# Setting up triangles in small parts between the state's steps, and two attention heads side by side on the array's columns

## The chip, the cores and the metric

The kernel runs on one core of one Trainium2 chip. The metric is the device time of one execution in microseconds (us); lower is better. A core has TensorE (PE; its weight loads are shown apart as PEld), VectorE (DVE), ScalarE (ACT), GpSimd (POOL) and SyncE (SP), which issues nearly all DMA transfers here. Each engine works through its own list of instructions in order.

## What is computed

Two layers over 2304 tokens (256 of context, 2048 latents on a grid 64 wide) of width 1024. In each layer a conditioning vector gives shift, scale and gate (`ada_modulation`); the normalised, modulated stream goes through one input projection into three groups of heads (A: gated delta rule, B: attention on a neighbourhood, C: gated linear attention), and their outputs, each gated, through one output projection.

```python
for i in range(DEPTH):
    sh, sc, gt = split(silu(c) @ w_mod[i] + b_mod[i])          # for c and for c_ctx
    m = layer_norm(x) * (1 + sc) + sh
    parts = split(m @ w_in[i])
    # group A, in chunks (of 64 tokens here, of 128 in the kernel), both directions, 4 heads of 128
    lmat = strict(k_beta @ k.T * decay);  u, w = solve(I + lmat, [v*beta, k_beta*exp(g)])
    for chunk: v_new = u - w @ S;  o = q_dec @ S + (q @ k.T * decay) @ v_new;  S = S * g_last + k_dec.T @ v_new
    # group B, 4 heads of 64: 8 x 16 window and 256 context keys
    p = softmax(concat(q @ k_window + bias, q @ k_ctx));  o = p @ concat(v_window, v_ctx)
    ...
    x = LN(alpha * x + gt * (concat(gated outputs) @ w_out[i]))
```

## The kernel before, in words

The tokens are 18 chunks of 128 (NT). Within a layer the stages stand in the program in this order: modulation (`stage_mod`, first layer only, with the first normalisation), a dense pass with group C, a dense pass for group B, a stage that makes tables and gates and the rest of the modulation vectors (`stage_mod` again: the gate row of this layer and, in layer 0, shift and scale of layer 1) together with two dense passes with a short convolution for group A, a dense pass for the gate of group A (here the *z pass*, lines 1260 and 1261), the delta rule with the attention, and the output projection.

`stage_mod` multiplies the two conditioning vectors (2 columns of weights, `e.cc`) with 512 columns of `w_mod` at a time: 8 matmuls per group of 512, four groups for shift and scale, two for the gate (line 104).

The delta rule (class `Gdn`) goes over the 4 heads in two pairs (`hp`) and over the chunks in both directions. Before a chunk can be used, its triangle has to be set up and inverted. This goes in batches of two groups of three chunks (`BATCHES`, three for each pair of heads, numbered 0 to 5): `prep` loads keys and decays, multiplies keys with keys and queries (line 849), and writes the triangle X and the matrix A (lines 853 to 860); `diagonal` takes the 32 x 32 blocks on the diagonals through DRAM, and inverts them by 30 eliminations, two VectorE instructions each (lines 913 and 914, a serial chain); `solve` loads the inverses back through DRAM, turns them (line 892) and puts the 128 x 128 inverse together on TensorE (`assemble`). Then `scan` runs steps: one *step* is one chunk in each direction for one pair of heads: state times keys (line 999), R (1003), X times R (1010), scale (1013), new part of the state (1017), state update (1022, or 1024 in the first step), output (1030, 1032). A step needs the state of the step before, so the 18 steps of a pair are a chain, and there are 36 steps in a layer.

`run` is a generator, advanced between the z pass and the two halves of the attention. Before the change it issues: prep 1, prep 2, solve 0 (then the z pass), then for k = 1 to 5 diagonal k and solve k as one piece, six steps, prep k+2; each piece in front of the steps that follow it.

The attention (class `Natten`) calls `attend` once for each 128 queries and pair of heads: 16 times in a pair for the latents, and, in layer 0, twice for the context: 68 times in all. The scores are evicted and made exponentials, transposed (lines 1229 and 1236), and multiplied with the values (line 1245): the transposed weights are the stationary operand (128 columns), 64 columns of v move, one head after the other, 2 + 4 products (2 + 3 at the upper and lower edge, 2 for the context) for each head. An fp32 matmul stands as two rows in the trace.

The order of instructions on each engine is made when the program is built: a list scheduler takes ready instructions, those that come earlier in the program first. So what is written earlier has the first claim on an engine, and later work (z pass, attention) fills what is left; on the chip each engine's order is then fixed.

Of the kernel before, what the change touches and what calls it, by code (L numbers as in the profile page):

```python
# [89 lines left out]
def stage_mod(e, pool, ps, tag, tt, bufs, w_mod, b_mod, modT, GT, parts, step):  # L90


    nc = e.nc
    w4 = w_mod.rearrange("(k p) n -> p k n", p=128)
    for n in parts:
        s = slice(512 * n, 512 * n + 512)
        b = pool.tile([2, 512], F32, tag="bm", name="b", bufs=2)
        nc.sync.dma_start(b, b_mod[s].partition_broadcast(2))
        p = ps.tile([2, 512], F32, tag=tag, name="p")
        for k in range(0, KD, step):  # L100
            w = pool.tile([128, step, 512], F32, tag="wm", name="w", bufs=bufs)
            nc.sync.dma_start(w, w4[:, k:k + step, s])
            for j in range(step):
                nc.tensor.matmul(p, e.cc[:, k + j], w[:, j], start=k + j == 0, stop=k + j == KD - 1)  # L104
        nc.vector.tensor_tensor(b, b, p, op=ALU.add)
        if n >= 4:
            nc.sync.dma_start(GT[:, 512 * (n - 4):512 * (n - 3)], b)
            continue
        pt = ps.tile([128, 4, 2], F32, tag=tt, name="pt")
        for j in range(4):  # L110
            nc.tensor.transpose(pt[:, j], b[:, j * 128:(j + 1) * 128], e.ident[0:2, 0:2])
        nc.vector.tensor_scalar(modT[:, 4 * n:4 * n + 4], pt, float(n >= 2), None, op0=ALU.add)
# [463 lines left out]
class Gdn:  # L576
# [179 lines left out]
    def start(self, ctx, dr, ps):  # L756
# [10 lines left out]
        self.XD[0] = self.prep(s, b, P, ps, "dn", ax)  # L767
        self.diagonal(P, *self.XD[0])
# [9 lines left out]
    def run(self):  # L778
# [5 lines left out]
        def prep(k):  # L784
            if k < len(self.BATCHES):
                hp, b = self.BATCHES[k]
                self.XD[k] = self.prep(self.st[hp], b, self.P1, self.ps, "pp", self.ax)

        def solve(k):
            hp, b = self.BATCHES[k]  # L790
            if k:
                self.diagonal(self.PM, *self.XD[k])
            self.solve(self.st[hp], b, *self.XD.pop(k))
# [7 lines left out]
        prep(1)  # L801
        prep(2)
        solve(0)
        yield
        for k in range(1, 6):
            solve(k)
            if k % 3:
                self.scan(self.st[k // 3], range(6 * (k % 3) - 6, 6 * (k % 3)))
            else:
                self.scan(self.st[k // 3 - 1], range(12, 18))  # L810
            prep(k + 2)
            if k == 3:
                yield
        self.scan(self.st[1], range(12, 18))
# [16 lines left out]
    def prep(self, s, batch, P, ps, tag, ax):  # L831
# [7 lines left out]
        for gi, g in enumerate(batch):  # L839
            A, X = zip(ax(), ax())  # L840
            for ci in range(3):
# [14 lines left out]
                for d in range(2):  # L856
# [3 lines left out]
                    nc.vector.tensor_tensor(A[d][:, ci], pk[:, :, 1], E[:, d], op=ALU.mult)  # L860
            for d in range(2):
# [15 lines left out]
        return n, LD, XD  # L877

    def diagonal(self, P, n, LD, XD):
# [4 lines left out]
        self.invert(P, M, n)  # L884
# [16 lines left out]
    def invert(self, P, M, n):  # L901
# [5 lines left out]
        for k in range(1, 31):  # L907
# [6 lines left out]
            nc.vector.tensor_tensor(o, o, tv, op=ALU.add)  # L914

# [50 lines left out]
    def scan(self, s, steps):  # L966
        nc = self.e.nc
        order = (list(range(NT)), [1, 0] + list(range(NT - 1, 1, -1)))
        for n in steps:
# [5 lines left out]
            for _ in zip(*both):  # L975
                pass
# [67 lines left out]
class Natten:  # L1044
# [162 lines left out]
    def attend(self, qs, keys, bias, nk, chunks, v, dst):  # L1207
# [25 lines left out]
        for a in range(2 if nk else 0):  # L1233
# [303 lines left out]
```

## Time and profile before

| | |
|---|---|
| time, median of 3 (lowest, highest) | 3989.75 us (3979.24, 4000.7) |
| profiled execution | 3995.01 us, its span 3992.9 us |
| busy PE, PEld, DVE, ACT, POOL | 91%, 78%, 63%, 42%, 20% |
| mean granted TensorE clock | 0.913 |
| DMA | 787.57 MB, mean 197 GB/s |

A busy PE means that a matmul is under way somewhere in the array's pipeline; a matmul's row is longer than the time until the next may start, so starts are compared, not durations. The granted clock is given as a share of full speed (1.0 is 2.4 GHz, 0.5 is 1.2 GHz). The layers are alike: layer 0 ends its delta rule and attention at 1794 us, layer 1 at 3745 us.

### The profile page before, as it was taken

What the parts mean: (1) busy time and instruction counts of PE and PEld (TensorE: products, weight loads), DVE (VectorE), ACT (ScalarE), POOL (GpSimd) and SP (SyncE); (2) the same over time, 40 slices, a digit from 0 to 9 for tenths busy, and PEclk for the clock granted to TensorE, in tenths of its full rate; (3) what the DMA queues carried; (4) which work ended last, traced back from release to release, by engine and by line L of the source; (5) the groups of instructions that cost most, each with busy time, mean ns of one, the idle gap of its engine ahead of it and who ended that gap; (6) DMA issues with size and microseconds to landing.
All of it is one profiled execution on the core that took longest, in us unless ns stands there. A gap on an engine that the chain in (4) does not pass through costs nothing.

```text
span 3992.9 us, 77074 instructions
## 1 busy us (share of the span) xinstructions
PE 3626.0 (91%) x27262; PEld 3113.1 (78%) x27262; DVE 2521.8 (63%) x7471; ACT 1660.0 (42%) x4387; POOL 810.2 (20%) x1182
## 2 busy tenths in 40 slices
PE   7999998899989999897898999999999898989788
PEld 3777787579977888896676778887998788879676
DVE  5465462668975676356875556527798766753587
ACT  4533231335433454446545333213454244545342
POOL 0121111210101332221232211112111132331133
PEclk8988988899999998898898888899999998988899
DMA  9843435876687876666647443268776887775753
GB/s 312 280 147 105 133 112 169 245 232 201 205 276 219 246 229 189 187 196 214 203 132 232 152 147 115 100 210 251 215 232 201 285 228 205 228 217 150 219 160 111
DMA packets 756088, 787.57 MB, mean 197 GB/s; under 512 B 190207, under 2 KB 665207, under 8 KB 755703
## 3 DMA queue, kind: packets, MB, share of 16 engines
q1 hardware_dynamic: 755702, 782.64, 63.6%
q8 instruction: 216, 3.54, 0.4%
q14 instruction: 170, 1.38, 0.1%
HBM read 548.41 MB, written 234.03 MB: 196 GB/s over the span
## 4 chain that ended last, share of the span: by engine, by line
PE 55%; DMA 19%; DVE 16%; ACT 4%; issue 3%; SPq 2%; POOL 0%; DVEq 0%; ACTq 0%; POOLq 0%
PE p L190 29%; DMA mm<-MS 3%; PE p L1245 3%; DMA gb<-GR 2%; PE p L104 2%; DMA kk<-KK 2%; DMA raw<-in_w_in 1%; PE py L190 1%; PE po L1030 1%; PE pk L999 1%; PE pv L1010 1%; DMA oa<-OA 1%; PE pd L1017 1%; PE pt L1236 1%; DVE y L1374 1%
## 5 line engine op out<-in xcount | busy, mean ns | idle before, releaser
L190 PE MATMUL p<-mm,wh 128*128 128x384 f32 (+1 forms) x3648 | 1004.0, 354 | 67.2 <-DMA mm<-MS 21.4
L190 PEld LDWEIGHTS p<-mm,wh 128*128 128x128 f32 (+1 forms) x3648 | 667.8, 192 | 133.7 <-DMA mm<-MS 36.9
L190 PE MATMUL p<-mm,wl 128*128 128x384 f32 (+1 forms) x1824 | 635.1, 350 | 1.8 <-DVE wl L182 1.8
L190 PE MATMUL p<-wh,mm 128*128 128x512 f32 (+1 forms) x1696 | 570.5, 409 | 14.5 <-DMA mm<-MS 4.9
L190 PEld LDWEIGHTS p<-wh,mm 128*128 128x128 f32 x1696 | 329.1, 197 | 92.0 <-DMA mm<-MS 8.4
L649 DVE SCALAR_TENSOR_TENSOR acc<-pre,cw,acc 128x384 f32<-128x384 f32 (+1 forms) x576 | 351.8, 629 | 39.2 <-ACT acc L647 35.8
L190 PEld LDWEIGHTS p<-mm,wl 128*128 128x128 f32 (+1 forms) x1824 | 348.9, 191 | 22.8 <-issue 14.6
L190 PE MATMUL p<-wl,mm 128*128 128x512 f32 (+1 forms) x848 | 341.5, 403 | 4.3 <-DVE wl L182 4.3
L190 PE MATMUL py<-wh,mh 128*128 128x512 f32 x544 | 221.7, 410 | 17.1 <-ACT mh L1360 13.2
L190 PE MATMUL py<-wh,ml 128*128 128x512 f32 x544 | 213.9, 405 | 8.7 <-DVE ml L1361 8.7
L190 PE MATMUL py<-wl,mh 128*128 128x512 f32 x544 | 217.8, 402 | 0.0
L190 PEld LDWEIGHTS p<-wl,mm 128*128 128x128 f32 x848 | 166.5, 196 | 38.5 <-DVE wl L182 4.8
L992 POOL TENSOR_TENSOR kd<-kk,eD 128x256 f32<-128x256 f32 x144 | 90.4, 628 | 476.4 <-DMA kk<-KK 225.6
L1224 ACT ACTIVATE w<-w,mn 128x696 f32<-128x696 f32 (+2 forms) x136 | 112.9, 830 | 143.9 <-DVE mn L1221 142.6
L1383 POOL TENSOR_TENSOR y<-y,g 128x1024 f32<-128x1024 f32 x32 | 77.5, 2423 | 416.0 <-ACT y L1382 416.0
L639 POOL COPY pre<-pre 128x4 f32<-128x4 f32 x120 | 75.0, 627 | 416.4 <-DVE acc L649 244.1
L913 DVE TENSOR_TENSOR tmp<-M 96x30 f32<-96x30 f32 (+4 forms) x360 | 127.1, 353 | 27.7 <-issue 11.3
L1245 PE MATMUL p<-v,wl 120*128 120x64 f32 (+1 forms) x960 | 141.1, 286 | 0.0
L853 DVE SCALAR_TENSOR_TENSOR gb<-gb,Gt,mats 128x128 f32<-128x128 f32 x288 | 86.7, 358 | 83.0 <-DMA gb<-GR 82.8
L1261 DVE SCALAR_TENSOR_TENSOR zt<-zt,p 128x256 f32<-128x256 f32 (+1 forms) x102 | 51.4, 506 | 138.8 <-ACT zt L1260 131.9
L190 PEld LDWEIGHTS py<-wh,mh 128*128 128x128 f32 x544 | 106.4, 196 | 41.4 <-ACT mh L1360 16.1
L914 DVE TENSOR_TENSOR M<-M,tmp 96x30 f32<-96x30 f32 (+4 forms) x360 | 130.4, 362 | 6.1
(307 smaller groups left out, 8021.8 us busy)
## 6 DMA issues: line engine op xcount, KB each, us to landing
mm<-MS SPq DMA_DIRECT2D x384, 384.0 KB
kk<-KK SPq DMA_DIRECT2D x144, 512.0 KB
MS<-mm SPq DMA_DIRECT2D x96, 384.0 KB
raw<-in_w_in SPq DMA_DIRECT2D x104, 256.0 KB
w<-in_w_mod SPq DMA_DIRECT2D x96, 256.0 KB
M<-m SPq DMA_DIRECT2D x36, 512.0 KB
mm<-M SPq DMA_DIRECT2D x96, 192.0 KB
KK<-kq SPq DMA_DIRECT2D x96, 192.0 KB
```

The lines of the kernel that those rows point to most:

```text
L104: nc.tensor.matmul(p, e.cc[:, k + j], w[:, j], start=k + j == 0, stop=k + j == KD - 1)
L190: e.nc.tensor.matmul(p, x(k), y(k), start=n == 0, stop=n == 3 * KD - 1)
L639: nc.gpsimd.tensor_copy(pre[:, 0:4], pre[:, m:m + 4])
L649: nc.vector.scalar_tensor_tensor(acc[:, :n], pre[:, k:k + n], w(kind, k), acc[:, :n], op0=ALU.mult, op1=ALU.add)
L853: nc.vector.scalar_tensor_tensor(E[:, d, h], gb[:, d, h], self.G[:, d, c, h0 + h:h0 + h + 1], e.mats[:, 1 + d], op0=ALU.subtract, op1=ALU.min)
L913: nc.vector.tensor_tensor(tv, col, row, op=ALU.mult)
L914: nc.vector.tensor_tensor(o, o, tv, op=ALU.add)
L992: nc.gpsimd.tensor_tensor(kd, kv[:, :, 0], self.eD[:, d, c, h0:h0 + 2].unsqueeze(2).to_broadcast([128, 2, 128]), op=ALU.mult)
L1224: nc.scalar.activation(w[:, a, 0:256 + nk], w[:, a, 0:256 + nk], AF.Exp, bias=m[:, a:a + 1], scale=-1.0, accum_out=sm[:, a:a + 1])
L1245: nc.tensor.matmul(p[:, a], l, r, start=j == 0, stop=j == len(parts) - 1)
L1261: nc.vector.scalar_tensor_tensor(th[:, :n], th[:, :n], 1.0, z, op0=ALU.add, op1=ALU.mult)
L1383: eng.tensor_tensor(y[:, s], y[:, s], self.g[:, 0, s], op=ALU.mult)
```

## The change

Three things change. (1) `scan` takes generators of other work and advances them between the sub-steps of its steps; `prep` yields after each chunk, and `invert` after each elimination, so that both are spread over the steps. The batches stand earlier in the program: the first three steps, with diagonal 1 between them, are issued before the z pass. (2) In `attend` the values are the stationary operand, 64 columns for each head, and the two heads' products stand side by side on the array's columns (tile positions 0 and 64), with 128 moving columns; the result comes out transposed, is copied by ScalarE and transposed back by one more matmul. (3) `stage_mod`, not named in the title, puts up to four groups of 512 on column positions 0, 32, 64 and 96, loads two groups by one transfer of 512 KB with half as many buffers, and finishes with one set of full transposes.

```diff
-    for n in parts:
-        s = slice(512 * n, 512 * n + 512)
...
-                nc.tensor.matmul(p, e.cc[:, k + j], w[:, j], start=k + j == 0, stop=k + j == KD - 1)
...
+    for k in range(KD):
+        for i0 in range(0, n, 2):
+            w = pool.tile([128, 2, 512], F32, tag="wm", name="w", bufs=bufs)
+            nc.sync.dma_start(w, w4[:, k, 512 * (n0 + i0):512 * (n0 + i0) + 1024].rearrange("p (i c) -> p i c", i=2))
+            for i in range(i0, i0 + 2):
+                nc.tensor.matmul(p[32 * i:32 * i + 2], e.cc[:, k], w[:, i - i0], start=k == 0, stop=k == KD - 1, tile_position=(0, 32 * i))
+    for i in range(n):
+        r = slice(32 * i, 32 * i + 2)
+        nc.vector.tensor_tensor(b[r], b[r], p[r], op=ALU.add)
...
@@ class Gdn, run
-        prep(1)
-        prep(2)
+        run = lambda *g: [None for x in g for _ in x]
+        run(prep(1))
         solve(0)
+        self.scan(self.st[0], range(3), diag(1))
+        run(prep(2))
         yield
-        for k in range(1, 6):
-            solve(k)
-            if k % 3:
-                self.scan(self.st[k // 3], range(6 * (k % 3) - 6, 6 * (k % 3)))
-            else:
-                self.scan(self.st[k // 3 - 1], range(12, 18))
-            prep(k + 2)
-            if k == 3:
-                yield
-        self.scan(self.st[1], range(12, 18))
+        solve(1)
+        self.scan(self.st[0], range(3, 6), diag(2))
+        solve(2)
+        self.scan(self.st[0], range(6, 12), prep(3), diag(3))
+        self.scan(self.st[0], range(12, 18), prep(4), diag(4))
+        yield
+        solve(3)
+        self.scan(self.st[1], range(3), prep(5))
+        solve(4)
+        self.scan(self.st[1], range(3, 6), diag(5))
+        solve(5)
+        self.scan(self.st[1], range(6, 18))
         yield
...
@@ invert, after each elimination; prep, after each chunk
+            yield
...
-    def scan(self, s, steps):
+    def scan(self, s, steps, *work):
+        parts = (x for w in work for x in w)
+        share = -(-48 // len(steps))
...
-            for _ in zip(*both):
-                pass
+            for i, _ in enumerate(zip(*both)):
+                if i:
+                    for _ in range(share // 6):
+                        next(parts, None)
+        for _ in parts:
+            pass
...
@@ attend
+        p = ps.tile([128, 128], F32, tag="t", name="p", bufs=2)
+        parts = [(128, lambda a, j=j: (self.vc[:, j], wc[:, a, j])) for j in range(2)] + [(k, lambda a, j=j, k=k: (v[:k, j], wl[a][:k, j])) for j, (_, k) in enumerate(chunks)]
+        for j, (k, f) in enumerate(parts):
+            for a in range(2):
+                c = slice(64 * a, 64 * a + 64)
+                l, x = f(a)
+                nc.tensor.matmul(p[c], l[:, c], x, start=j == 0, stop=j == len(parts) - 1, tile_position=(0, 64 * a))
+        pT = P.tile([128, 128], F32, tag="pT", name="pT", bufs=1)
+        nc.scalar.copy(pT, p)
         p = ps.tile([128, 2, 64], F32, tag="t", name="p", bufs=2)
-        for a in range(2):
-            c = slice(64 * a, 64 * a + 64)
-            parts = [(wc[:, a, j], self.vc[:, j, c]) for j in range(2)] + [(wl[a][:k, j], v[:k, j, c]) for j, (_, k) in enumerate(chunks)]
-            for j, (l, r) in enumerate(parts):
-                nc.tensor.matmul(p[:, a], l, r, start=j == 0, stop=j == len(parts) - 1)
+        nc.tensor.transpose(p.rearrange("p h d -> p (h d)"), pT, e.ident)
...
@@ layer
-                for n in (range(2), range(2, 4)):
-                    stage_mod(e, P, ps, "pa", "pm", 11, i["w_mod"][0], i["b_mod"][0], layers[0].modT, GT, n, 1)
-                    next(p1, None)
+                next(p1)
+                stage_mod(e, P, ps, "pa", "pm", 6, i["w_mod"][0], i["b_mod"][0], layers[0].modT, GT, range(4))
+                next(p1, None)
...
-                                    stage_mod(e, P1, ps, "dn", "dn", 4, i["w_mod"][j], i["b_mod"][j], layers[j].modT, layers[j].GT, n, 1)
+                                    stage_mod(e, P1, ps, "dn", "dn", 2, i["w_mod"][j], i["b_mod"][j], layers[j].modT, layers[j].GT, n)
```

**VectorE, layer 0, where the first step updates its state.** M is the batch of blocks that is being inverted, S the state, zt the z pass, R a step. Before, the last eliminations of diagonal 1 and diagonal 2 and the whole z pass stand ahead of the first step:

```order
L914 TENSOR_TENSOR M<-M,tmp 96x28x3
L913 TENSOR_TENSOR tmp<-M 96x58
L914 TENSOR_TENSOR M<-M,tmp 96x29x2
L913 TENSOR_TENSOR tmp<-M 96x30
L914 TENSOR_TENSOR M<-M,tmp 96x30
L1261 SCALAR_TENSOR_TENSOR zt<-zt,p 128x512
L1024 COPY S_13302<-pd 128x256
L1024 COPY S_13304<-pd 128x256
L1003 SCALAR_TENSOR_TENSOR R<-pk,neG,kk 128x128 x4
```

Now the eliminations of diagonal 1 stand between the two directions' updates:

```order
L930 TENSOR_TENSOR tmp<-M 96x198
L931 TENSOR_TENSOR M<-M,tmp 96x22x9
L1049 COPY S_12100<-pd 128x256
L930 TENSOR_TENSOR tmp<-M 96x184
L931 TENSOR_TENSOR M<-M,tmp 96x23x8
L930 TENSOR_TENSOR tmp<-M 96x168
L931 TENSOR_TENSOR M<-M,tmp 96x24x7
L930 TENSOR_TENSOR tmp<-M 96x150
L931 TENSOR_TENSOR M<-M,tmp 96x25x6
L930 TENSOR_TENSOR tmp<-M 96x130
L931 TENSOR_TENSOR M<-M,tmp 96x26x5
L1049 COPY S_12102<-pd 128x256
```

The first steps moved into the z pass: ten of its eighteen rows in layer 0 now come behind the first state update, none before. Ahead of the first attention result of layer 0 stand six steps now and five before.

**TensorE, layer 0, one call of `attend`.** pt are transposes of the weights, p the value product, pl the next call's scores. Before:

```order
L1236 MATMUL pt<-ident,w 120x128 x3
L1236 MATMUL pt<-ident,w 80x128
L1010 MATMUL pv<-R,X 128x128 x2
L1017 MATMUL pd<-v,kd 128x128 x2
L1245 MATMUL p<-vc,wc 128x64 x2
L1245 MATMUL p<-v,wl 128x64 x4
L1245 MATMUL p<-vc,wc 128x64 x2
L1245 MATMUL p<-v,wl 128x64 x4
```

Now:

```order
L1261 MATMUL pt<-ident,w 120x128 x3
L1261 MATMUL pt<-ident,w 80x128
L1204 MATMUL pl<-kh,q 128x440
L1205 MATMUL pl<-kl,qz 128x440
L1272 MATMUL p<-wc,vc 64x128 x4
L1272 MATMUL p<-wl,v 64x128 x8
L1204 MATMUL pl<-kh,q 128x440
L1205 MATMUL pl<-kl,qz 128x440
L1276 MATMUL p<-ident,pT 128x128
```

Twelve products stay twelve, with half the stationary and twice the moving columns; the transpose back stands behind the next call's scores.

## Rows read from the trace of the kernel before

**Rows 1.** The page's chain that ended last: by engine, by line.

```profile
PE 55%; DMA 19%; DVE 16%; ACT 4%; issue 3%; SPq 2%; POOL 0%; DVEq 0%; ACTq 0%; POOLq 0%
PE p L190 29%; DMA mm<-MS 3%; PE p L1245 3%; DMA gb<-GR 2%; PE p L104 2%; DMA kk<-KK 2%; DMA raw<-in_w_in 1%; PE py L190 1%; PE po L1030 1%; PE pk L999 1%; PE pv L1010 1%; DMA oa<-OA 1%; PE pd L1017 1%; PE pt L1236 1%; DVE y L1374 1%
```

**Rows 2.** Windows: length, busy PE, PEld, DVE, ACT, POOL; granted clock, DMA share, GB/s.

```profile
10.00:45.00 35.00, 32.08 (x81) 6.02 (x79) 15.49 (x41) 3.56 (x8) 0.00 (x0) 1.00 1.04 354
735.00:855.00 120.00, 118.48 (x511) 72.87 (x511) 73.70 (x169) 35.62 (x88) 31.28 (x44) 1.00 0.94 273
2735.00:2780.00 45.00, 44.91 (x199) 29.27 (x198) 42.34 (x90) 18.90 (x41) 15.37 (x26) 1.00 0.98 285
1115.00:1200.00 85.00, 73.51 (x323) 59.33 (x322) 58.96 (x219) 26.84 (x73) 7.46 (x21) 0.94 0.97 313
1200.00:1282.00 82.00, 79.21 (x683) 63.24 (x681) 53.84 (x153) 23.53 (x59) 14.07 (x37) 0.92 0.68 211
1282.00:1345.00 63.00, 54.41 (x556) 48.48 (x556) 30.47 (x100) 26.29 (x74) 22.06 (x51) 0.92 0.95 260
1345.00:1620.00 275.00, 250.63 (x2409) 231.41 (x2403) 184.80 (x606) 134.95 (x373) 74.95 (x152) 0.91 0.76 217
1620.00:1669.00 49.00, 45.03 (x412) 40.33 (x412) 12.55 (x38) 23.85 (x65) 15.13 (x38) 0.72 0.54 147
3227.00:3287.00 60.00, 54.11 (x532) 48.24 (x530) 39.27 (x127) 24.78 (x70) 23.70 (x55) 0.89 0.96 268
3563.00:3626.00 63.00, 56.35 (x456) 51.36 (x455) 17.95 (x57) 27.03 (x70) 12.87 (x35) 0.65 0.34 96
```

**Rows 3.** Windows of line 1022 alone (four state updates a step): length, busy, count.

```profile
1345.00:1620.00 275.00, 19.93 (x68) 0.91 0.76 217
1620.00:1669.00 49.00, 1.38 (x6) 0.72 0.54 147
1669.00:1790.00 121.00, 12.68 (x44) 1.00 0.66 202
3563.00:3626.00 63.00, 0.95 (x5) 0.65 0.34 96
3715.00:3743.00 28.00, 3.46 (x13) 0.82 0.67 205
```

**Rows 4.** Windows of line 1249 alone (one row ends one attend call).

```profile
1620.00:1669.00 49.00, 0.87 (x3) 0.72 0.54 147
1669.00:1790.00 121.00, 3.45 (x12) 1.00 0.66 202
3563.00:3626.00 63.00, 1.13 (x4) 0.65 0.34 96
```

**Rows 5.** Timeline of PE: start, us, line, shapes, count.

```profile
19.41 4.03 PE L104 MATMUL p<-w,cc 128*2 128x512 f32 x9
258.06 0.43 PE L533 MATMUL pS<-v,kd 128*32 128x64 f32 x16
1222.57 0.86 PE L962 MATMUL px<-X,z 64*64 64x64 f32 x12
1358.39 0.83 PE L1245 MATMUL p<-v,wl 120*128 120x64 f32 x6
3593.41 1.92 PE L1245 MATMUL p<-v,wl 120*128 120x64 f32 x8
```

**Rows 6.** Groups by line: busy us, mean ns, then idle before and its releasers.

```profile
L104 PE MATMUL p<-w,cc 128*2 128x512 f32 x192 | 95.4, 613 | 11.6 <-DMA w<-in_w_mod 11.5
L853 DVE SCALAR_TENSOR_TENSOR gb<-gb,Gt,mats 128x128 f32<-128x128 f32 x288 | 86.7, 358 | 83.0 <-DMA gb<-GR 82.8
L858 DVE SCALAR_TENSOR_TENSOR X<-pk,nW,gb 128x128 f32<-128x128 f32 x288 | 86.7, 342 | 19.9 <-PE pk L849 9.6 <-ACT gb L855 6.1 <-DMA far<-X 3.5
L860 DVE TENSOR_TENSOR A<-pk,gb 128x256 f32<-128x256 f32 x144 | 59.1, 413 | 2.5 <-PE po L1030 2.5
L913 DVE TENSOR_TENSOR tmp<-M 96x30 f32<-96x30 f32 (+4 forms) x360 | 127.1, 353 | 27.7 <-issue 11.3 <-DMA x<-XD 9.8 <-DMA M<-LD 0.4
L914 DVE TENSOR_TENSOR M<-M,tmp 96x30 f32<-96x30 f32 (+4 forms) x360 | 130.4, 362 | 6.1
```

More of the change, by code (lines that the diff above doesn't have):

```diff
@@ L87, in stage_cond, with stage_mod @@
     return cc
-def stage_mod(e, pool, ps, tag, tt, bufs, w_mod, b_mod, modT, GT, parts, step):
+def stage_mod(e, pool, ps, tag, tt, bufs, w_mod, b_mod, modT, GT, parts):
     nc = e.nc
     w4 = w_mod.rearrange("(k p) n -> p k n", p=128)
-    for n in parts:
-        s = slice(512 * n, 512 * n + 512)
[L97 to L103, printed above, removed]
-                nc.tensor.matmul(p, e.cc[:, k + j], w[:, j], start=k + j == 0, stop=k + j == KD - 1)
[L105 to L112, printed above, removed]
@@ new lines, in stage_mod @@
+    n0, n = parts[0], len(parts)
+    b = pool.tile([128, 512], F32, tag="bm", name="b", bufs=1)
+    nc.gpsimd.memset(b, 0.0)
+    for i, x in enumerate(parts):
+        nc.sync.dma_start(b[32 * i:32 * i + 2], b_mod[512 * x:512 * x + 512].partition_broadcast(2))
+    p = ps.tile([128, 512], F32, tag=tag, name="p")
+    for k in range(KD):
[4 more added lines that the diff above has]
+                nc.tensor.matmul(p[32 * i:32 * i + 2], e.cc[:, k], w[:, i - i0], start=k == 0, stop=k == KD - 1, tile_position=(0, 32 * i))
@@ new lines, in stage_mod @@
+    for i in range(n):
+        r = slice(32 * i, 32 * i + 2)
+        nc.vector.tensor_tensor(b[r], b[r], p[r], op=ALU.add)
+    if n0 >= 4:
+        for i in range(n):
+            nc.sync.dma_start(GT[:, 512 * (n0 - 4 + i):512 * (n0 - 3 + i)], b[32 * i:32 * i + 2])
+        return
+    pt = ps.tile([128, 4, 128], F32, tag=tt, name="pt")
+    for j in range(4):
+        nc.tensor.transpose(pt[:, j], b[:, j * 128:(j + 1) * 128], e.ident)
+    for i in range(n):
+        m = modT[:, 4 * (n0 + i):4 * (n0 + i) + 4]
+        nc.vector.tensor_scalar(m, pt[:, :, 32 * i:32 * i + 2], float(n0 + i >= 2), None, op0=ALU.add)
@@ L766, in start @@
         ax = lambda: [P.tile([128, 3, 2, 128], F32, tag=t, name=t) for t in "AX"]
-        self.XD[0] = self.prep(s, b, P, ps, "dn", ax)
-        self.diagonal(P, *self.XD[0])
+        for _ in self.prep(s, b, P, ps, "dn", ax, 0):
+            pass
+        for _ in self.diagonal(P, *self.XD[0]):
+            pass
     def weights(self, hp):
@@ L784, in prep, with diag @@
         def prep(k):
-            if k < len(self.BATCHES):
-                hp, b = self.BATCHES[k]
-                self.XD[k] = self.prep(self.st[hp], b, self.P1, self.ps, "pp", self.ax)
+            hp, b = self.BATCHES[k]
+            yield from self.prep(self.st[hp], b, self.P1, self.ps, "pp", self.ax, k)
+        def diag(k):
+            yield from self.diagonal(self.PM, *self.XD[k])
         def solve(k):
             hp, b = self.BATCHES[k]
-            if k:
-                self.diagonal(self.PM, *self.XD[k])
             self.solve(self.st[hp], b, *self.XD.pop(k))
@@ L829, in store, with prep @@
         self.e.nc.sync.dma_start(far["AX".index(t)], x.rearrange("p c h t -> p (c h t)"))
-    def prep(self, s, batch, P, ps, tag, ax):
+    def prep(self, s, batch, P, ps, tag, ax, key):
         e, nc = self.e, self.e.nc
@@ L876, in prep @@
             nc.sync.dma_start(LD[b].rearrange("u j i -> j u i"), xd[32 * b:32 * b + 32].rearrange("p g u i -> p (g u) i"))
-        return n, LD, XD
+        self.XD[key] = n, LD, XD
+        yield
     def diagonal(self, P, n, LD, XD):
@@ L883, in diagonal @@
         nc.sync.dma_start(M, LD.rearrange("b u j i -> (b u) j i"))
-        self.invert(P, M, n)
+        yield from self.invert(P, M, n)
         nc.sync.dma_start(XD.rearrange("b u j i -> (b u) j i"), M)
@@ L914, in invert @@
             nc.vector.tensor_tensor(o, o, tv, op=ALU.add)
+            yield
     def assemble(self, X, d, xc, xt, i):
@@ L974, in scan @@
             both = [self.step(s, d, order[d][n], n) for d in range(2)]
-            for _ in zip(*both):
-                pass
+            for i, _ in enumerate(zip(*both)):
[3 more added lines that the diff above has]
+        for _ in parts:
+            pass
     def step(self, s, d, c, n):
```

## Prediction

> **What bounds the kernel now.** I read the chain of the page first, then stretches, then counts of steps and attention calls, then rows of TensorE. The chain is a mixture: TensorE has 55% of it, DMA 19%, VectorE 16%, and the dense products (line 190) alone 29%, which the change leaves as they are [rows 1]. Of what it touches, the value product (line 1245) has 3% and the modulation (line 104) 2%. So no single wait goes; each stage needs its own reading.
>
> - Modulation. From 10 to 45 us all engines wait for DMA: its share is 1.04. The second place, 735 to 855 us, has TensorE busy in 118.5 of 120 us and DMA at 0.94; the third, 2735 to 2780, has both full (0.98) [rows 2].
> - The stretch before the steps (z pass with prep and solve) starts with DMA at 0.97 for 85 us, then 0.68 for 82 us; the first steps, 1282 to 1345, run at 0.95 [rows 2].
> - Middle steps: 68 updates of line 1022 in 275 us are 17 steps of 16.2 us. Late steps: 44 updates in 121 us are 11 steps of 11.0 us with 12 attention calls among them; the last 13 updates, 3.25 steps with no attention, take 28 us, 8.6 a step [rows 3, 4]. So a step has a floor of about 9 us by its own chain of waits, an attention call hidden in it costs about 2, and the other 5 of a middle step come from triangles.
> - Where the chunks of a pair's last batch are needed, the steps stop: in 1620 to 1669 us only 6 updates, in 3563 to 3626 only 5, while 3 and 4 attention calls end, at a granted clock of 0.72 and 0.65 [rows 2 to 4].
>
> **The change part by part.** The sum is made against the profiled execution, 3995.0 us (a span of 3992.9 and 2.1 around it), which lies 0.13% above the median of the runs, 3989.75.
>
> *Modulation.* A row with 512 moving columns starts (4.03 - 0.59) / 8 = 0.43 us after the one before (the duration of one is 0.59) [rows 5]. Layer 0's second place has 6 groups x 8 products x 2 rows = 96 rows, 41 us; layer 1's has 32, 13.7 us. In the new order the products stand in pairs on two column groups between dense products, seldom four together, so a half is saved: 20.6 and 6.9 us of TensorE. But the bytes stay, and DMA there is free for only 0.06 x 120 = 7 and 0.02 x 45 = 1 us [rows 2]. I take -8 and -1, by the nearer row, which is DMA's. Bounds: -27.5 if DMA gives way, and +11.5 if TensorE is held up for the larger transfers once more as long as it is now for all of w_mod [rows 6]. At the start the transfers set the time (35 us at 1.04), TensorE finishes sooner, but three more evictions follow the last transfer: 0, between -5 and +4.
>
> *Value product.* Now a row of 128 stationary and 64 moving columns starts (0.83 - 0.28) / 5 = 0.11 us after another: the weight load sets it. 64 stationary columns: (0.86 - 0.22) / 11 = 0.058 us. Moving 128 fp32 columns alone would take 0.43 / 4 = 0.107, but two column groups share that if they run side by side. The trace has such a case: line 533 puts 64 moving columns on four groups in turn, and its rows start (0.43 - 0.22) / 15 = 0.014 us apart, where 0.43 / 8 = 0.054 would be a group alone: four at once [rows 5]. So a row comes to about 0.056. All calls have 960 + 544 = 1504 such rows, 168 us; 84 after, and 68 transposes back at 0.11 add 7: 77 us less TensorE work. Its share of the path: line 1245 is 3% of the chain, 124 us by the page, so at most 57. On the other side the floor of a step is not TensorE's, an attention call costs a late step only 2 us, and the new copy and transpose lengthen each call (by up to about 1 us, less the 1.3 it saves). Between 0 and -57 I take -20, nearer to the rows of the late steps.
>
> *Steps moved ahead.* Five more steps now lie beside the z pass. By busy DMA the three stretches from 1115 to 1345 us hold 82 + 56 + 60 = 198 us in 230 [rows 2]; at the 0.95 of the first steps this takes 208. So -20 in each layer, -40 (the first steps of layer 1 run at 0.96 too). Bounds: 0, where SyncE's queue holds the step's loads behind those of the z pass, and -32 each at a share of 1.0.
>
> *Steps left.* From step 6 to the last, the order has ten more pieces (rows of A) of triangle set-up in layer 0 and eight in layer 1, since set-up that stood ahead of the first step moved behind it. A piece is half of 4 x 0.358 + 4 x 0.342 + 2 x 0.413 us, 1.8 of VectorE [rows 6]: 18 and 14 us more. The eliminations are as many (30 pairs x 0.72 us = 21 a batch [rows 6]), now about six to a step, 4.3 us, which fits between a step's 3.2 us of VectorE and a call's 2.5 within the floor. Spreading hides some of the pieces; +24 of the 32. Bounds: 0 and +32.
>
> *The stop at the last batch.* Its round trip through DRAM and the assembly stay, and its diagonal is still not done when the steps reach it: twelve eliminations of diagonal 5 follow step 5 of layer 0's second pair. In layer 0 six attention calls stand in that stop, before three; in layer 1 five, before four. I take 0 as the steps would have had to carry the same calls; its other end is the third rival.
>
> Sum: 3995 - 9 - 20 - 40 + 24 = 3950. Less the 5 us that the profiled run is above the median: **3945**.
>
> **The rivals.**
>
> *Relief is paid in full.* TensorE is the largest part of the chain, and in 1345 to 1620 it is busy 251 of 275 us [rows 1, 2]. Then -27 for modulation, -57 for the value product, -64 for the steps moved: 3995 - 148 + 24 - 5 = 3866. Against it: DMA at 0.94 to 0.98 where modulation stands, and the floor of a step.
>
> *Nothing to be seen.* DMA already takes the z pass, and the triangles' pieces take in later steps what is gained: -9 - 5 - 20 + 24 leaves 3985 less 5: 3980 to 3985.
>
> *The stop grows (slower).* Attention calls in the stops of before took 49 / 3 and 63 / 4, 16 us each, at a low clock: (1.92 - 0.42) / 7 = 0.21 us for a row of line 1245, twice its usual time [rows 2 to 5]. If calls there go one after the other like this ahead of the assembly in TensorE's list, six and five take 96 and 80 us where 49 and 63 stood: +64, and the three calls ahead of step 6 and of the second pair's first step in layer 0 another +20 or so. With the rest at -45 - 5: about 4030. It decides when the stops grow by more than 70 us. For it speaks that such stops are the longest; against it, that half of the value product's rows is gone there too.
>
> *The pair doesn't run side by side.* Then each row costs its load and its moving columns, 0.058 + 0.107 = 0.165 against 0.11: some +80 us of TensorE, at 124/168 of it on the path +59 instead of -20: 4024. Line 533's rows [rows 5] speak against it. The Trainium skill (TensorE: Matmul & The Clock Gate, Part 3: Packing small matmuls — row/col tiling) says that a weight load overlaps a matmul in flight only where the row group differs; the two heads use the same rows, so by that rule this rival would be the forecast. The trace disagrees: line 533's four groups share all 128 rows too and run 0.014 us apart.
>
> **How the numbers follow.** Forecast 3945, its own range 3915 to 3975: 0.42. Relief in full, about 3866: 0.15. Nothing to be seen, 3980 to 3985: 0.22. The stop grows, about 4030: 0.17. No side by side, 4024: 0.04. About 0.5%, 20 us, is what a measurement can tell here: faster is below 3970, slower above 4010. Faster: 0.42 x 0.85 + 0.15 + 0.03 = 0.54. Slower: 0.17 + most of 0.04 + 0.02 of the third: 0.22. The same: 0.24. The range, 3868 to 4028, leaves out half of the first rival and half of the third; it holds the sum's bounds but for those where all fall on one side.
>
> **What would show it.** Line 1245's successor at 0.056 us a row, in about 84 us; if the rows start 0.1 or more apart, the fourth rival is at work. The first step some 40 us earlier with DMA near 0.95 through the z pass; if that stretch ends no earlier, the second. Middle steps with six eliminations and a call at 11 to 13 us instead of 16. The stops: in layer 0 under 60 us the forecast stands, at 80 or more the third rival. In 735 to 855 the modulation should leave TensorE idle while DMA stays at 0.95; if TensorE stays full, the first. The forecast is wrong if the steps still take 16 us, or if the two layers' delta-rule stretches together gain less than 15 us or more than 80.

## The result and the profile after

The changed kernel takes 4023.44 us (median of 6 runs, 4011.86 to 4031.7) where the kernel before took 3992.51 (6 runs beside them): a ratio of 1.007, 95% interval 1.0045 to 1.0095. It is slower; the prediction said faster, 3945. The profiled execution has a span of 4028.1 us (before: 3992.9) and a mean granted clock of 0.898 (before: 0.913).

The chain that ended last, by engine and by line, answers to [rows 1]:

```profile
PE 55%; DMA 20%; DVE 14%; ACT 5%; issue 3%; SPq 2%; POOL 1%; DVEq 0%; ACTq 0%; POOLq 0%
```

The shares hardly move: the value product (now line 1272) has 2% where it had 3%, the modulation (now line 107) is no longer among the first. So the loss doesn't show as a share; it has to be found in stretches. Windows of the changed kernel, columns as in [rows 2]:

```profile
10.00:52.00 42.00, 22.60 (x76) 3.81 (x76) 23.12 (x66) 6.57 (x17) 0.00 (x0) 0.80 0.90 314
735.00:855.00 120.00, 108.02 (x550) 83.21 (x549) 76.79 (x190) 40.78 (x101) 31.06 (x48) 0.96 0.94 270
2755.00:2800.00 45.00, 44.00 (x228) 33.89 (x229) 40.87 (x87) 20.03 (x44) 13.95 (x25) 0.96 0.94 284
1110.00:1200.00 90.00, 73.96 (x532) 60.30 (x531) 56.42 (x204) 28.93 (x82) 14.03 (x35) 0.87 0.88 285
1200.00:1278.00 78.00, 76.60 (x527) 62.78 (x527) 46.55 (x143) 21.12 (x52) 13.96 (x32) 1.00 0.81 252
1250.00:1289.00 39.00, 38.78 (x338) 32.26 (x339) 22.04 (x64) 11.71 (x31) 6.30 (x16) 0.90 0.68 203
1310.00:1354.00 44.00, 37.49 (x383) 30.82 (x381) 10.71 (x31) 22.56 (x63) 15.43 (x39) 0.69 0.59 157
1511.00:1547.00 36.00, 30.64 (x351) 25.85 (x349) 20.81 (x58) 18.37 (x54) 11.24 (x25) 0.76 0.87 241
1590.00:1618.00 28.00, 28.00 (x282) 24.98 (x283) 10.79 (x37) 15.55 (x42) 5.50 (x14) 0.62 0.55 161
1646.00:1702.00 56.00, 49.45 (x553) 39.73 (x554) 24.99 (x78) 35.12 (x96) 13.87 (x37) 0.91 0.39 107
```

The first three are the modulation, the next two the stretch up to the end of the z pass, with steps 0 to 2 in it, and the last five are the gaps in front of steps 3, 6, 18, 21 and 24 of layer 0 (from the last state update of the step before, line 1047, to its own). Those are the steps that first need the chunks of batches 1 to 5. The kernel before has one long gap among them, 49 us at step 24 [rows 2]; here there are five, at a granted clock of 0.62 to 0.91. Their sum, read in the same way in both traces (us):

| | steps 3, 6, 18, 21, 24 | steps 39, 42, 54, 57, 60 (layer 1) |
|---|---|---|
| before | 8 + 20 + 8 + 17 + 49 = 102 | 12 + 35 + 13 + 20 + 63 = 145 |
| after | 39 + 44 + 36 + 28 + 56 = 203 | 37 + 23 + 19 + 29 + 57 = 165 |

Step 0 ends at 1200 us where it ended at 1282, 81 us earlier; step 5 is 35 ahead, step 17 25 ahead, step 23 26 behind, and the last step 20 behind. In layer 1 step 0 is 32 ahead, step 5 20 behind and the last step 30 behind. In layer 0 the steps after the first lose 101 us against before, and the five gaps grew by the same 101. In layer 1 they lose 62 and the gaps grew by 20; the other 42 lie in steps 1 and 2 (34 us where 20 stood), 4 and 5 (40 and 27), and 19, 20, 22 and 23 (58 and 45). What holds those was not traced.

What ends last in a gap is seen on VectorE. Its rows around step 24, first before, where line 914 is an elimination, 892 turns the inverse that came back from DRAM, and 1022 is the state update (start, us, engine, line; in brackets the idle time ahead and what ended it):

```profile
1606.31 0.21 DVE L914 TENSOR_TENSOR M<-M,tmp 96x30 f32<-96x30 f32 x1
1619.75 0.59 DVE L1022 SCALAR_TENSOR_TENSOR S<-S,eT,pd 128x128 f32<-128x128 f32 x2
1631.81 0.98 DVE L892 STREAM_TRANSPOSE x<-x 128x768 f32<-128x768 f32 x1 [2.33 <-DMA x<-XD]
1667.96 1.13 DVE L1022 SCALAR_TENSOR_TENSOR S<-S,eT,pd 128x128 f32<-128x128 f32 x4 [0.59 <-PE pd L1017]
```

and after (931, 909 and 1047 are the same lines):

```profile
1645.74 0.59 DVE L1047 SCALAR_TENSOR_TENSOR S<-S,eT,pd 128x128 f32<-128x128 f32 x2
1659.05 0.20 DVE L931 TENSOR_TENSOR M<-M,tmp 96x30 f32<-96x30 f32 x1
1669.57 0.98 DVE L909 STREAM_TRANSPOSE x<-x 128x768 f32<-128x768 f32 x1 [4.55 <-DMA x<-XD]
1701.02 1.12 DVE L1047 SCALAR_TENSOR_TENSOR S<-S,eT,pd 128x128 f32<-128x128 f32 x4 [0.89 <-PE pd L1042]
```

Before, the last elimination ends 13 us ahead of step 23's last update, and the gap holds only the rest of the way. After, it ends 13 us behind that update, and the whole way lies in the gap. The text on the change says that the batches stand earlier in the program; that holds against the z pass, not against the steps. The set-up of batch 3 stood ahead of step 6 and now runs between steps 6 and 11, that of batch 5 stood ahead of step 18 and now runs between steps 18 and 20. In the traces the first rows of A of batches 3, 4 and 5 are written at 1369, 1402 and 1566 us, where 1303, 1387 and 1490 stood. The chain of waits of the changed kernel, in order of time (start, us, what), shows that way:

```profile
1658.08 0.23 DVE M L931
1659.85 4.45 DMA XD<-M
1665.85 3.60 DMA x<-XD
1669.57 0.99 DVE x L909
1670.60 1.30 PE pz L948 x24
1679.28 1.27 PE p L1272 x10
1692.59 0.70 PE px L980 x12
1696.68 1.09 PE pv L1035 x8
```

Elimination, out to DRAM, back, turned, assembled on TensorE (between the attention's products), then the step: 42 us from the last elimination to the state update.

The same reading at all batches: by how much the turned inverse (line 892, then 909) starts ahead of the last update of the step before the one that needs it (us; a minus is behind):

| step of the layer | 3 | 6 | 18 | 21 | 24 |
|---|---|---|---|---|---|
| before, layer 0 | 57 | 36 | 93 | 40 | -12 |
| after, layer 0 | 32 | -14 | 1 | 19 | -24 |
| before, layer 1 | 37 | 6 | 87 | 30 | -20 |
| after, layer 1 | 11 | 12 | 9 | 15 | -21 |

Step 18 is the clearest. Batch 3's inverse is turned, before and after, at

```profile
1443.46 0.98 DVE L892 STREAM_TRANSPOSE x<-x 128x768 f32<-128x768 f32 x1 [0.73 <-DMA x<-XD]
```

```profile
1509.53 0.98 DVE L909 STREAM_TRANSPOSE x<-x 128x768 f32<-128x768 f32 x1
1510.62 0.59 DVE L1047 SCALAR_TENSOR_TENSOR S<-S,eT,pd 128x128 f32<-128x128 f32 x2
```

and step 17 ends at 1536 before, at 1511 after. What follows the turning, assembly and step, takes 31 us at step 24 (1670 to 1701); a lead shorter than that leaves a gap. Much of this way is attention, whose products stand between those of the assembly in TensorE's list. In e8 below, the last batch comes when the attention is done, and there the same way takes 17 us (1731.0 to 1747.8), at a granted clock of 0.50, with none of the attention's value products (line 1271 there) in it:

```profile
1731.01 0.98 DVE L908 STREAM_TRANSPOSE x<-x 128x768 f32<-128x768 f32 x1 [2.46 <-DMA x<-XD]
1747.79 0.61 DVE L1046 SCALAR_TENSOR_TENSOR S<-S,eT,pd 128x128 f32<-128x128 f32 x2 [15.80 <-PE pd L1041]
1731.00:1748.00 17.00, 0.00 (x0) 0.00 (x0) 0.50 0.19 67
```

By this, an estimate, some 14 us of the 31 at step 24 are attention work, which has to be done at some time; what the new order adds is that more of the way lies in the gap. Step 3 is a case of its own: there the assembly is what waits, for products of the z pass (line 198), which have 59% of the chain from 1250 to 1289 us:

```profile
by line: PE p L198 59.0%; PE pz L948 8.4%; PE px L954 6.1%; PE pv L1035 5.1%; PE pd L1042 5.1%; PE px L980 5.1%; PE pz L974 4.0%; PE pk L1024 2.8%; PE pt L963 1.6%; DVE zt L1292 1.6%; PE po L1057 1.1%; PE po L1055 1.1%; issue 0.1%
```

TensorE is idle for little of a gap, since attention calls fill it. Its idle time in front of an assembly's first product (line 930, then 948; busy, mean ns, idle and what ended it) doubles over the execution, by 10 us, 4 of them put down to the turned inverse (lines 892 and 909); before and after:

```profile
L930 PE MATMUL pz<-x,X 32*32 32x32 f32 x1152 | 50.8, 199 | 9.8 <-DVE x L892 8.6 <-ACT z L931 1.2
```

```profile
L948 PE MATMUL pz<-x,X 32*32 32x32 f32 x1152 | 55.6, 210 | 19.9 <-DVE x L909 12.3 <-DVE r L1278 7.2
```

### The profile page after: what moved, and what is told of

The parts are those of the page before. It is cut to its first block, busy times and chain, and to the rows that moved or that the text cites. A ratio compares the mean times of both kernels' runs of the same rounds, so it can differ in the third digit from the quotient of the medians.

```text
span 4028.1 us, 77136 instructions
## 1 busy us (share of the span) xinstructions
PE 3577.9 (89%) x27306; PEld 3051.3 (76%) x27306; DVE 2507.9 (62%) x7471; ACT 1678.4 (42%) x4455; POOL 813.4 (20%) x1186
## 4 chain that ended last, share of the span: by engine, by line
PE 55%; DMA 20%; DVE 14%; ACT 5%; issue 3%; SPq 2%; POOL 1%; DVEq 0%; ACTq 0%; POOLq 0%
PE p L198 29%; DMA mm<-MS 3%; PE py L198 2%; PE p L1272 2%; DMA gb<-GR 2%; DMA kq<-KK 1%; PE pv L1035 1%; DMA raw<-in_w_in 1%; PE pd L1042 1%; PE po L1055 1%; PE pk L1024 1%; PE pk L864 1%; DMA tb<-TB 1%; PE pt L1261 1%; DVE mix L1382 1%
## 5 line engine op out<-in xcount | busy, mean ns | idle before, releaser
L198 PE MATMUL p<-wh,mm 128*128 128x512 f32 (+1 forms) x1696 | 568.9, 408 | 28.8 <-DMA mm<-MS 14.2
L1246 DVE CUSTOM_DVE_ANT_0 w<-pl,tb,mn 128x440 f32<-128x440 f32 (+1 forms) x128 | 81.8, 639 | 113.2 <-PE pl L1205 92.3
L187 ACT CAST wh<-raw 128x512 fp32r<-128x512 f32 (+3 forms) x144 | 76.5, 554 | 137.8 <-DMA raw<-in_w_in 115.3
L1038 ACT ACTIVATE v<-pv,Wt 128x128 f32<-128x128 f32 x288 | 88.4, 364 | 109.4 <-PE pv L1035 108.5
```

The source lines that it names most:

```text
L187: eng_hi.copy(hi, src)
L198: e.nc.tensor.matmul(p, x(k), y(k), start=n == 0, stop=n == 3 * KD - 1)
L1038: nc.scalar.activation(v[:, h], pv[:, h], AF.Copy, scale=sc(self.W, h))
L1246: nc.vector.tensor_tensor_reduce(w[:, a, 256:256 + nk], pl, bias[:, a], scale=1.0, scalar=mn[:, 0, a:a + 1], op0=ALU.add, op1=ALU.min, acc ...
```

## The experiments

Medians; the ratio is to the kernel before on the same chip. "Stretch" is the time from the first column block of the z pass to the last step, layer 0 + layer 1, in the profiled execution, which for e9 is 16 us below the median of its runs and for e13 28 above; "gaps" are the ten gaps of the table above.

| run | time | ratio, 95% | stretch | gaps |
|---|---|---|---|---|
| before | 3992.51 | | 648 + 647 | 102 + 145 |
| after | 4023.44 | 1.007 (1.0045 to 1.0095) | 681 + 656 | 203 + 165 |
| e1 heads, modulation | 3960.75 | 0.9925 (0.9900 to 0.9950) | 631 + 634 | 85 + 131 |
| e2 new order alone | 4086.00 | 1.0232 (1.0199 to 1.0266) | 706 + 691 | 201 + 166 |
| e3 heads alone | 3978.31 | 0.9957 (0.9937 to 0.9978) | 620 + 645 | 78 + 128 |
| e4 modulation alone | 4010.53 | 1.0039 (1.0016 to 1.0062) | 645 + 658 | 86 + 126 |
| e5 not spread | 4020.86 | 1.0060 (1.0033 to 1.0087) | 679 + 647 | 204 + 162 |
| e6 first half | 3982.32 | 0.9969 (0.9944 to 0.9995) | 649 + 635 | 152 + 133 |
| e7 second half | 4021.92 | 1.0070 (1.0045 to 1.0095) | 669 + 662 | 131 + 143 |
| e8 lead | 4110.97 | 1.0286 (1.0238 to 1.0334) | 718 + 704 | 136 + 123 |
| e9 after, no own inverse | 3924.89 | 0.9842 (0.9796 to 0.9888) | 592 + 605 | 105 + 87 |
| e10 e1, no own inverse | 3914.83 | 0.9815 (0.9766 to 0.9865) | 600 + 596 | 70 + 65 |
| e11 old places, spread | 3967.53 | 0.9948 (0.9917 to 0.9980) | 625 + 656 | 90 + 134 |
| e12 ready ahead | 3996.35 | 1.0009 (0.9980 to 1.0037) | 658 + 662 | 147 + 153 |
| e13 batch 5 earlier | 3947.39 | 0.9897 (0.9863 to 0.9931) | 633 + 645 | 95 + 121 |
| e14 batches 4, 5 earlier | 3949.16 | 0.9908 (0.9873 to 0.9943) | 636 + 628 | 98 + 112 |

**The parts apart (e1 to e4).** e1 leaves the class `Gdn` as before and takes the new `attend` and `stage_mod`; e2 takes only the new `Gdn`; e3 only `attend`; e4 only `stage_mod`.

> The change without its schedule of triangles and steps: two heads side by side and the new modulation, the delta rule as before. Theory A (the loss is the new places of the batches, each inverse arrives when its step already waits): 3945 to 3970, faster than before by 20 to 45 us, since the modulation gave 13 us in layer 0 and the value product is shorter. Rival B (the attention call with its copy and transpose back is what costs): 4000 or more. Rival C (neither alone, only together): 3985 to 4000.

> The new schedule alone, attention and modulation as before. Theory A: slower than before by 35 to 70 us, 4030 to 4060, with steps 3, 6, 18, 21 and 24 of a layer each waiting for an inverse that ends under 15 us before it. Rival B: 3970 to 3990, no slower than before. Rival C: 3990 to 4005.

> Two heads side by side alone. Theory A: 3960 to 3985, and rows of the value product at most 0.06 us apart at full clock. Rival B: 4005 to 4030. If the column groups did not run side by side, the rows would start 0.1 us or more apart.

> The new modulation alone. Theory A: 3975 to 3988 (12 us gained by the end of the convolutions of layer 0, about nothing in layer 1 and at the start). Rival C: the 12 us are given back before the steps, 3990 to 3995.

The new order is the loss: with it 4023, without it 3961; alone +92, more than expected. The heads alone bring 16 us. The modulation alone was expected level or better and costs 16; on top of the heads (e3 to e1) it brings 13 by the ratios, 18 by the medians. In the same way the heads bring some 45 on top of the modulation (e4 to e1). The modulation's own stretch is shorter in e4's trace too (the convolution ends 8 us earlier); why the time is not, stays open. The parts do not add up; that each moves instructions of the others in the order is the likely reason, and was not shown.

**Place or spreading (e5 to e8).** e5 keeps the new places but issues each piece whole:

```diff
-        parts = (x for w in work for x in w)
...
+        for w in work:
+            for _ in w:
+                pass
```

e6 has the new places for batches 0 to 2 and the old ones for 3 to 5; e7 the reverse; e8 spreads as the change does, with more lead for each batch:

```diff
-        self.scan(self.st[0], range(3, 6), diag(2))
-        solve(2)
-        self.scan(self.st[0], range(6, 12), prep(3), diag(3))
-        self.scan(self.st[0], range(12, 18), prep(4), diag(4))
-        yield
-        solve(3)
...
+        self.scan(self.st[0], range(3), diag(2))
+        solve(2)
+        self.scan(self.st[0], range(3, 9), prep(3), diag(3))
+        solve(3)
+        self.scan(self.st[0], range(9, 14), prep(4), diag(4))
+        solve(4)
+        self.scan(self.st[0], range(14, 18), prep(5))
+        yield
...
```

> The changed kernel with one thing different: the preps and diagonals stand at the same places between the steps, but each is issued whole ahead of the steps of its stretch, not spread between their sub-steps. Theory A (the places: a batch is solved right in front of the step that needs it, so its round trip through DRAM and its assembly lie bare): little moves, 4000 to 4030, and the gaps at steps 3, 6, 18, 21 and 24 stay between 25 and 60 us; the whole pieces have only the lead of three to six steps. Rival D (the spreading: the eliminations, one or two to a sub-step, end later than they would in a piece and so the inverse comes late): the time falls to about that of the two other parts without the new schedule, 3955 to 3980.

> The changed kernel with batches 3, 4 and 5 put back where they stood before (whole pieces: prep 3 ahead of step 6, diagonal and solve 3 ahead of step 12, 4 ahead of the second pair, 5 ahead of its step 6); batches 0 to 2 and the three steps ahead of the z pass stay as changed. Theory A: the gaps at steps 18 and 21 fall under 20 us, and what is lost between the last step of the first pair and step 24 (58 us in layer 0, 21 in layer 1) comes back: 3945 to 3975. Rival F (what is lost is lost in the first half, where the gaps at steps 3 and 6 eat the 81 us that the first step gained): over 4000.

> The reverse of e6: batches 0 to 2 as before (no steps ahead of the z pass), batches 3 to 5 spread and late as changed. Theory A: the gaps at steps 18, 21 and 24 are those of the changed kernel (28 to 56 us); against the run with heads and modulation alone (3961) it costs the 58 + 21 us of that stretch: 4020 to 4045. Rival F: 3955 to 3980.

> All three parts, with the work spread between sub-steps as in the change, but each batch ends earlier: solve 2 three steps ahead of its step 6, solve 3 nine, solve 4 seven and solve 5 four steps ahead of theirs, and solve 1 ahead of the first steps. Theory A: the gaps at steps 3, 6, 18, 21 are under 20 us, the one at 24 under 35, and the time is 3930 to 3965, below the run with heads and modulation alone or level with it. Rival D (spreading itself costs): the gaps go but the steps lengthen, 3985 to 4030.

e5 settles the spreading: the same time and, in sum, the same gaps with whole pieces. By the ratios, the second half costs most (e7 lies 58 us above e1), the first 18 (e6, 7 us above its expected range); together that is more than the 58 of both, so the halves do not add up either. e8 went against the theory: the gaps at 3, 6, 18 and 21 are indeed 20, 15, 9 and 18 us, but it is the slowest of all. Its last batch is prepared at 1647 us where e1 has it at 1480, and TensorE stands still for it in both layers:

```profile
1732.04 1.92 PE L947 MATMUL pz<-x,X 32*32 32x32 f32 x33 [13.85 <-DVE x L908]
3738.45 1.92 PE L947 MATMUL pz<-x,X 32*32 32x32 f32 x33 [30.47 <-DVE x L908]
```

It also has new gaps of 90 and 104 us in front of steps 11 and 47, where triangles that were put away are loaded back. Step 10 ends at 1400 us; the load is issued at 1483 and releases step 11's product (SyncE, then TensorE):

```profile
1483.55 0.34 SPq L838 DMA_DIRECT2D X<-far  x1
```

```profile
1486.90 0.71 PE L1034 MATMUL pv<-R,X 128*128 128x128 f32 x4 [0.79 <-DMA X<-far]
```

What holds the load (a free slot, or its place in SyncE's queue) was not separated. So here the lead of some batches went with a later last batch and with the new gaps.

**The wait itself (e9, e10).** In both, no assembly waits for its own batch: every solve reads the layer's first inverses, which have DRAM buffers of their own. All eliminations and transfers still run.

```diff
-            self.solve(self.st[hp], b, *self.XD.pop(k))
+            n, _, XD = self.XD.pop(k)
+            if k == 0:
+                self.XD0 = XD
+            self.solve(self.st[hp], b, n, None, self.XD0)
...
```

> The changed kernel, but every solve takes the inverses of the layer's batch 0, which are long there, in place of its own batch's (all eliminations and both transfers still run; the triangles of the other batches get wrong blocks). So only the wait for the inverse goes. Theory A' (in the new places a batch's own inverse and its way through DRAM end last in front of steps 3, 6, 18, 21, 24): the gaps there shrink to 10 to 30 us and the time falls by 50 or more, to 3940 to 3975. Rival G (what stands in the stops is the assembly and the attention's and z pass's products on TensorE, and the inverse would be hidden by them): less than 25 us, over 3998.

> The same edit on the kernel with heads and modulation and the old order of batches (e1, 3961): its inverses come 55 to 100 us before most steps that need them. Theory A': only the stop at the last batch shrinks, 10 to 30 us, 3930 to 3950, so that the old and the new places differ by less than 25 us when nothing waits for an inverse. Rival G: the two differ by 60 as before.

Without a wait for the inverse the changed kernel gains 99 us and e1 46, both more than expected, and the two orders come together: 3925 and 3915, the stretches 1197.5 and 1196.7 us, where with their own inverses they are 1338 and 1265. Of the 63 us that the new order costs (58 by the ratios), 10 are left (11), and the intervals of e9 and e10 overlap. So most of the cost comes from the wait for a batch's own inverse. (The expectation for e10 puts e1's inverses 55 to 100 us ahead of most steps; in e1's trace only two of ten leads are over 55, and most lie between 4 and 40.) In three of e9's gaps, at steps 6, 18 and 24 (windows, all engines), the length and the clock show it:

```profile
1295.00:1321.00 26.00, 22.82 (x288) 20.76 (x288) 3.65 (x12) 10.51 (x31) 11.06 (x27) 0.65 0.79 243
1502.00:1514.00 12.00, 11.97 (x169) 9.94 (x167) 9.13 (x30) 8.35 (x25) 3.42 (x8) 1.00 0.81 238
1589.00:1602.00 13.00, 12.60 (x114) 10.75 (x113) 6.47 (x26) 8.15 (x23) 2.63 (x4) 1.00 0.94 331
```

Step 3 keeps its gap (39 us), as it should, since the z pass makes it. Two limits. Whether the other values in the triangles move the clock was not tested. And the order of instructions is built anew for e9, so attention calls move too. One row of line 1280 (1283 in e9) ends one call; the gaps at steps 6 and 18, first after, then e9:

```profile
1310.00:1354.00 44.00, 0.87 (x3) 0.69 0.59 157
1511.00:1547.00 36.00, 0.86 (x3) 0.76 0.87 241
```

```profile
1295.00:1321.00 26.00, 0.00 (x0) 0.65 0.79 243
1502.00:1514.00 12.00, 0.28 (x1) 1.00 0.81 238
```

The pair shows one thing more. Step 0 of layer 0 ends 63 us earlier in e9 than in e10 (1192.5 and 1255.5), step 3 only 14 (1277.7 and 1292.1), the last step 10. In layer 1, counted from the end of layer 0's steps, it is 64, 26 and nothing. So even where nothing waits for an inverse, the head start of the new order hardly stays.

**Looking for a better order (e11 to e14).** All have heads and modulation.

```diff
 e11:   self.scan(self.st[0], range(6), diag(2)); run(prep(3)); solve(2)   # and so on: diagonal k over the steps ahead of solve k
 e12:   run(prep(1), prep(2)); solve(0); run(diag(1)); solve(1); self.scan(self.st[0], range(3), diag(2)); yield; solve(2)
 e13:   self.scan(self.st[0], range(12, 15)); run(prep(5)); self.scan(self.st[0], range(15, 18))   # diagonal and solve 5 behind scan(range(3)) of pair 2
 e14:   as e13, diag(4) in scan(range(12, 15)), solve(4) ahead of step 15, diagonal and solve 5 ahead of pair 2's first step
```

> Heads and modulation, solves and preps at their old places, but diagonals 2 to 5 spread over the six steps ahead of their solve instead of standing whole behind them. Theory A' (spreading costs nothing by itself, late places do): 3945 to 3970, level with 3961 or a little better, since the inverses come earlier. Rival D: the steps lengthen, over 3985.

> Three steps ahead of the z pass as in the change, but with batches 1 and 2 prepared, and batch 1 solved, ahead of them, and diagonal 2 spread over them; batches 3 to 5 at their old places. Theory A' (the first half loses what it gains because prep 2 stands behind step 2): gaps at steps 3 and 6 under 25 us and a time under e1's 3961, 3925 to 3955. If the z pass and the steps share a full DMA, nothing is gained: 3955 to 3975. Rival F (the steps ahead themselves cost): as the run with the first half, 3975 to 3990.

> Heads and modulation with the old order, but prep 5 three steps earlier (ahead of step 15 in place of behind step 17) and diagonal and solve 5 three steps earlier (ahead of step 21). If the place alone sets the wait, the gap at step 24 falls under 25 us in both layers and the time to 3935 to 3955 (e1: 3961). If the slots for triangles are what prep 5 waits for, prep 5 runs no earlier than in e1 (from 1480 us) or the steps wait for slots: 3955 to 3990.

> The same, and diagonal 4 spread over steps 12 to 14, solve 4 ahead of step 15, solve 5 ahead of the second pair's first step. By place alone: gaps at 18, 21 and 24 all under 20 us, 3925 to 3950. By slots: a stop of 50 us or more in the steps 12 to 18, as in e8, and over 3985.

e11: spreading at the old places is neither gain nor loss. e12 missed: the gaps at 3 and 6 did close (24 and 22 us), but prep 3 then starts at 1343 us where e1 has it at 1289, every later inverse is late, and the gaps at 21 and 24 are 29 and 54. Taking steps ahead moves the wait to a later batch. e13 and e14 are 13 and 12 us faster than e1 by their medians, with intervals that overlap e1's. The gap at step 24 of layer 0 is 40 and 45 us, longer than e1's 28; in layer 1 it is 22 and 26 against 43. In layer 0 prep 5 begins at 1475 and 1489 us in them, where e1 has 1480, though it was put three steps earlier: something other than its place holds it, and what (the slots are the guess) stays open. e13 has the lowest time of the complete versions, 0.9897 of before, not clear of e1, e11 and e14.

## Why the prediction was wrong

- *Modulation, -9.* Right in its own stretch: 735 to 855 leaves TensorE 12 us idle with DMA at 0.94, as forecast, and the products take about half the time: four rows 1.03 us, where four rows 0.43 us apart would take 1.88:

```profile
743.58 1.03 PE L107 MATMUL p<-w,cc 128*2 128x512 f32 x4 [1.00 <-DMA w<-in_w_mod]
```

  The stage from the second pass to the convolution's end is 10 us shorter in layer 0 (426 us where 436 stood) and level in layer 1 (380 and 379); at the start the vectors are ready 5 us later (51.0 us where 45.9 stood), 1 more than my bound, and this is made up by the end of the second pass. In time the part brought 13 to 18 or cost 16, depending on what stood beside it; no step of mine saw that.
- *Value product, -20.* Right alone: 16 us (e3, 9 to 25 by its interval). The -20 was picked between 0 and -57, and beside the new modulation it is some 45, so the hit is partly luck; the mechanism is as forecast. The rows run as forecast, two heads side by side, (0.66 - 0.27) / 7 = 0.056 us apart (0.27 is one row of line 1276):

```profile
1397.66 0.66 PE L1272 MATMUL p<-wc,vc 128*64 128x128 f32 x8 [0.20 <-ACT wc L1255]
1398.15 1.05 PE L1272 MATMUL p<-wl,v 120*64 120x128 f32 x16
1356.74 0.27 PE L1276 MATMUL p<-ident,pT 128*128 128x128 f32 x1
```

  One column group alone would need 0.107 us a row for its moving columns, by the forecast's 0.43 / 4. So the fourth rival falls, and the rule that stood for it does not hold here: the two heads share their rows and run side by side.
- *Steps moved ahead, -40: failed too.* The first step is 81 us earlier in layer 0, and in layer 1 52, counted from the end of layer 0's steps, more than forecast (e1, without the new order, has 23 and -2). But I booked this as a gain that stays, and e9 and e10 show that it hardly does even without a wait. I counted on free DMA, five steps beside the z pass and a share of 0.95. The traces have three steps there. In layer 0 the share is 0.82 where 0.80 stood, the z pass takes 149 us instead of 137, steps 1 and 2 take 50 us instead of 25, and step 3 waits for the z pass's products. The z pass, first after, then before (windows, all engines):

```profile
1129.00:1278.00 149.00, 136.06 (x997) 111.94 (x998) 92.48 (x297) 43.57 (x114) 27.75 (x66) 0.94 0.82 256
```

```profile
1142.00:1279.00 137.00, 127.30 (x849) 101.40 (x849) 94.93 (x302) 37.91 (x97) 19.66 (x52) 0.94 0.80 250
```

- *Steps left, +24.* This cost is not seen: from step 7 on, outside the gaps, the steps of both layers take 674 us, before 675. The forecast's 16.2 us for a middle step was misread: 1345 to 1620 holds 18 steps, since step 18's update stands on another line, 15.3 each, with the gaps of steps 6, 18 and 21 among them. For steps 7 to 17 alone, the trace before has 171 and 162 us (layers 0 and 1), e1 162 and 163, after 157 and 163: 14.2 us a step in layer 0, above the 11 to 13 forecast. After, between the gaps:

```profile
1354.00:1511.00 157.00, 13.39 (x46) 0.95 0.82 239
1702.00:1790.00 88.00, 9.81 (x33) 0.96 0.71 211
```

- *The stop at the last batch, 0: the step that failed most.* It was worked out for step 24 alone, and there it comes out against before: 56 and 57 us where 49 and 63 stood. That is partly luck, since in e1 these stops are 28 and 43: the other parts took 41 us off and the order put as much back. The error is that I counted one stop for each pair of heads. Before, batches 2 and 5 alone were solved right in front of the step that needs them; in the new order batches 1 to 5 all are, and each step taken ahead makes the next batch due earlier. The five gaps grew by 101 and 20 us against before, by 118 and 34 against e1. The three terms of the order came to -16 together; after stands 63 above e1. By e9 and e10 some 50 of these 63 are the wait for the inverse; the other 10 lie within the intervals of the two runs. The 16 that the order was to bring are not seen even there.

The signs that I named were too weak for this. The stop of layer 0 stayed under 60 us, by which the forecast stood. The sign that held is the last one: the two delta-rule stretches lost 42 us (681 + 656 for 648 + 647).

Of the rivals the fourth has the nearest time (4024) by chance, since its rows are not there. The third (4030) is right in part. It had six and five attention calls in the two long stops and three ahead of steps 6 and 18 of layer 0, and so many end there; they do stand between the products of the assembly. But it priced them at 16 us each, so that the two long stops would grow by 64 us; together they grew by 1, about 10 us a call. At steps 6 and 18, which it priced at 20, the gaps grew by 52, because inverses that had been 36 and 93 us ahead came 14 us late and 1 us ahead. How much those gaps would be with the late inverse and no attention call in them was not run.

## What to carry to other kernels

When work is moved between the links of a serial chain, list for every link what it needs, when that ends and how long its way is (here 42 us from the last elimination to the update), before and after; a link moved ahead makes its inputs due sooner. In this kernel a gain at the head of the chain did not last, because the next inputs had no lead left. And price a wait by an experiment that gives the consumer older data: one pair of runs told what the changes of order could not.

## What the runs showed that was not expected

Some gaps go with a low TensorE clock although TensorE is shown busy for 85 to 100% of them: in the gaps of layer 0 at steps 6, 18 and 21 the granted clock was 0.69, 0.76 and 0.62, at steps 3 and 24 it was 0.90 and 0.91, close to the mean of the execution. Two of the three gaps of e9 shown above ran at 1.00. In the profiled executions the mean clock fell from 0.912 (e1) to 0.898 (after) and was 0.916 in e9. For the same 27306 instructions TensorE is shown busy for 3537.6 us in e1 and 3577.9 in after: of the 77 us between the two spans, 40 are longer busy time and 37 idle time. How much of the loss is the clock and how much the wait was not separated further.
